# Rotary embedding on one core: whole-batch transfers, an earlier first load, and five tiles added or multiplied by other engines

## The chip, the cores and the metric

The kernel runs on one core of a Trainium2 chip. A core has five engines with queues of their own: PE (TensorE, matrix products into PSUM), DVE (VectorE), ACT (ScalarE), POOL (GpSimd) and SP (SyncE, used here only to issue transfers). Sixteen DMA engines move data between the main memory (HBM) and the on-chip memory (SBUF). PSUM is a second, smaller on-chip memory that PE writes and that DVE and ACT can read and write.

The metric is the device time of one execution in microseconds (us). Times are medians over several executions; what is profiled is one execution, whose span runs from its first to its last instruction.

## The reference

`x` has the shape (8, 2048, 8, 64), that is batch, position, head and feature, in float32: 33.5 MB. `cos` and `sin` are (2048, 32). For every position the two halves of a head's 64 features are rotated:

```python
x1 = x[..., : x.shape[-1] // 2]
x2 = x[..., x.shape[-1] // 2 :]
cos = cos[None, :, None, :]
sin = sin[None, :, None, :]
out1 = x1 * cos - x2 * sin
out2 = x1 * sin + x2 * cos
return np.concatenate([out1, out2], axis=-1)
```

The kernel must read 33.5 MB and write 33.5 MB, and do four multiplications and two additions for each pair.

## The kernel before

Each of the 128 partitions holds 16 consecutive positions of a batch. A position is `HD` = 512 floats (8 heads of 64), so a partition's row of one batch is 8192 floats (32 KB) that lie together in memory. A *slab* is half of such a row, 4096 floats or 16 KB in each of 128 partitions: 2 MB. There are 16 slabs, first the left halves of all eight batches, then the right halves. Ten slab buffers (`NBUF`) lie in SBUF. A slab is worked on in *units* of 2048 floats per partition (`UNIT`); the first slab in four smaller and larger pieces, and the last one too.

For each piece, `rotate` (line 97) issues four operations:

- POOL multiplies the second half of every head by sin and writes it where the first half's result goes, with the sign in the table (`nsin` is minus sin, line 91), and the first half by sin likewise: two multiplications of half the piece, line 107, into `t2` (SBUF, three buffers).
- DVE multiplies the whole piece by cos into `t1` (PSUM, one buffer), line 112. Its table `cos_ps` lies in PSUM, line 92.
- DVE adds `t1` and `t2` and writes the sum over the piece of `x`, line 117.

So the slab buffer becomes the output buffer. ACT issues the store of a slab once it is finished (line 127; the last slab is stored in four pieces), and SP issues the load of the slab ten places on, when the buffer's store has landed (lines 80 and 132). The tables are loaded first, sin on SP's queue (line 86) and cos on ACT's (line 87), then the first ten slabs on SP's queue. The semaphores are put in by the framework from the order in which tiles are written and read. A tile of a pool with `bufs` buffers takes the place of the tile `bufs` places before it, and waits until everything that reads that one has ended.[...]

Of the kernel before, what the change touches and what calls it, by code (L numbers as in the profile page):

```python
# [2 lines left out]

# [4 lines left out]


@with_exitstack  # L10
def kernel(
    ctx: ExitStack,
    tc: tile.TileContext,
    x: bass.AP,
    cos: bass.AP,
    sin: bass.AP,
    out: bass.AP,
):
    nc = tc.nc
    f32 = mybir.dt.float32  # L20
    PSUM = bass.MemoryType.PSUM

    B, S, H, D = x.shape
    Dh = D // 2
    P = 128
    HD = H * D
    R = S // P

    SL = 8
    n_half = R // SL  # L30
    SLAB = SL * HD
    UNIT = 4 * HD
    NBUF = 10

    xv = x.rearrange("b (q r) h d -> b q (r h d)", q=P)
    ov = out.rearrange("b (q r) h d -> b q (r h d)", q=P)
    cos_src = cos.rearrange("(q r) d -> q r d", q=P)
    sin_src = sin.rearrange("(q r) d -> q r d", q=P)

    const_pool = ctx.enter_context(tc.tile_pool(name="const", bufs=1))  # L40
    tab_pool = ctx.enter_context(tc.tile_pool(name="tab", bufs=1, space=PSUM))
    t1_pool = ctx.enter_context(tc.tile_pool(name="t1p", bufs=1, space=PSUM))
    xpool = ctx.enter_context(tc.tile_pool(name="xpool", bufs=NBUF))
    t2_pool = ctx.enter_context(tc.tile_pool(name="t2p", bufs=3))

    cos_sb = const_pool.tile([P, R, Dh], f32, tag="cb")
    sin_sb = const_pool.tile([P, R, Dh], f32, tag="sb")
    nsin = const_pool.tile([P, R, Dh], f32, tag="ns")
    cos_ps = tab_pool.tile([P, R, Dh], f32, tag="cp")

    slabs = [(b, l) for l in range(n_half) for b in range(B)]
    last = len(slabs) - 1
    xts = {}

    def cuts(i):
        if i == 0:
            return [HD, HD, 2 * HD, UNIT]
        return [SLAB]

    def pieces(i):  # L60
        if i == 0:
            return [HD, HD, 2 * HD, UNIT]
        if i == last:
            return [UNIT, 2 * HD, HD, HD]
        return [UNIT, UNIT]

    def stores(i):
        return pieces(i) if i == last else [SLAB]

    def spans(sizes):  # L70
        lo = 0
        for n in sizes:
            yield lo, n
            lo += n

    def load(i):
        b, l = slabs[i]
        xt = xpool.tile([P, SLAB], f32, tag="xt", name=f"xt{i}")
        for lo, n in spans(cuts(i)):
            nc.sync.dma_start(  # L80
                out=xt[:, lo : lo + n],
                in_=xv[b, :, l * SLAB + lo : l * SLAB + lo + n],
            )
        xts[i] = xt

    nc.sync.dma_start(out=sin_sb, in_=sin_src)  # L86
    nc.scalar.dma_start(out=cos_sb, in_=cos_src)
    for i in range(NBUF):
        load(i)

    nc.scalar.mul(nsin, sin_sb, -1.0)  # L91
    nc.vector.tensor_copy(cos_ps, cos_sb)  # L92

    def rep(a, n):
        return dataclasses.replace(a, ap=[a.ap[0][:], a.ap[1][:], [0, n], a.ap[-1][:]])

    def rotate(i, lo, n):
        b, l = slabs[i]
        xt = xts[i][:, lo : lo + n]
        r0 = l * SL + lo // HD  # L100
        nr = n // HD
        t1 = t1_pool.tile([P, n], f32, tag="t1")
        t2 = t2_pool.tile([P, n], f32, tag="t2")
        xu = xt.rearrange("p (g u d) -> p g u d", u=2, d=Dh)
        t2u = t2.rearrange("p (g u d) -> p g u d", u=2, d=Dh)
        for u, tab in ((1, sin_sb), (0, nsin)):
            nc.gpsimd.tensor_mul(  # L107
                out=t2u[:, :, u, :].rearrange("p (r h) d -> p r h d", h=H),
                in0=xu[:, :, 1 - u, :].rearrange("p (r h) d -> p r h d", h=H),
                in1=rep(tab[:, r0 : r0 + nr, :], H),  # L110
            )
        nc.vector.tensor_mul(  # L112
            out=t1.rearrange("p (r k d) -> p r k d", r=nr, d=Dh),
            in0=xt.rearrange("p (r k d) -> p r k d", r=nr, d=Dh),
            in1=rep(cos_ps[:, r0 : r0 + nr, :], 2 * H),
        )
        nc.vector.tensor_add(out=xt, in0=t1, in1=t2)  # L117

    for i, (b, l) in enumerate(slabs):
        done = 0  # L120
        st = list(spans(stores(i)))
        for lo, n in spans(pieces(i)):
            rotate(i, lo, n)
            done = lo + n
            while st and st[0][0] + st[0][1] <= done:
                slo, sn = st.pop(0)
                nc.scalar.dma_start(
                    out=ov[b, :, l * SLAB + slo : l * SLAB + slo + sn],
                    in_=xts[i][:, slo : slo + sn],
                )  # L130
        if i >= 1 and i - 1 + NBUF <= last:
            load(i - 1 + NBUF)


# [1 line left out]
_INS = ['x', 'cos', 'sin']  # L136
_OUTS = [((8, 2048, 8, 64), 'float32')]


# [23 lines left out]
```

## Time and profile before

| what | us |
|---|---|
| median of 9 runs (lowest, highest) | 164.95 (164.57, 165.22) |
| the profiled execution, device time | 164.97 |
| its span, first to last instruction | 163.2 |
| DVE busy in it | 148.8 |
| POOL busy in it | 147.7 |
| ACT busy in it | 1.9 |
| one DVE operation on 128x2048 (L112, L117) | 2.295, 2.292 |
| one POOL operation on 128x1024 (L107) | 2.33 |
| ACT, 128x512 (L91) | 0.63 |
| a 256 KB store at the end, issue to landing | 2.6 |

The profile's page gives the busy time of each engine, then the span in 40 slices of 4.08 us each (the busy share in tenths of every engine, and what the DMA engines moved), then a chain of waits: from the last instruction back to what released it, again and again, so that the shares say which engine held up the end. After that come groups of like instructions, by line: the engine, the operation, the tile written and the tile read, the number, the busy time in all, the mean duration of one in ns, and the engine's idle time just before them with what ended it. The timeline lists instructions in order of start: start, duration, engine, line.

The transfers moved 67.65 MB, 415 GB/s over the span.

### The profile page before, as it was taken

The page shows a single profiled execution, that of the slowest core. Times are in us where ns is not written, and L with a number is a line of the kernel's source. Part 1 is how long each engine was busy: PE and PEld are TensorE (multiplying, and loading weights), DVE is VectorE, ACT ScalarE, POOL GpSimd, SP SyncE. Part 2 cuts the span into 40 slices and gives each one's busy share as a digit, 9 for nine tenths or more (in the row PEclk, how much of TensorE's full clock was granted, in tenths as well). Part 3 has the DMA queues.
Part 4 walks back from the last instruction along what each step waited for, and adds up shares of the span by engine and source line. Part 5 has one row for each costly group of instructions (what it writes and reads, how often), then busy time and mean ns, then how long its engine had stood idle before and what let it go on. Part 6 is the DMA issues. An engine that isn't in the chain of part 4 may idle for free.

```text
span 163.2 us, 331 instructions
## 1 busy us (share of the span) xinstructions
DVE 148.8 (91%) x73; ACT 1.9 (1%) x2; POOL 147.7 (91%) x76
## 2 busy tenths in 40 slices
DVE  0687999999999999999999999999999999999992
ACT  3100000000000000000000000000000000000000
POOL 0799999999999999999999989999998998989720
DMA  5999999999999999999999999999999999999994
GB/s 157 359 444 434 402 394 434 434 434 426 434 434 418 442 434 430 430 434 428 418 442 438 426 426 442 428 418 442 442 418 426 446 426 422 442 430 430 426 410 193
DMA packets 5763, 67.65 MB, mean 415 GB/s; under 512 B 641, under 2 KB 641, under 8 KB 1665
## 3 DMA queue, kind: packets, MB, share of 16 engines
q1 hardware_dynamic: 2880, 33.82, 49.7%
q10 hardware_dynamic: 2880, 33.82, 48.6%
q14 instruction: 3, 0.02, 0.0%
HBM read 34.08 MB, written 33.55 MB: 414 GB/s over the span
## 4 chain that ended last, share of the span: by engine, by line
DVE 84%; DMA 7%; POOL 3%; issue 2%; SPq 1%; DVEq 0%; POOLq 0%
DVE xt L117 43%; DVE t L112 41%; DMA xt<-in_x_dram 7%; POOL t L107 3%; SPq L80 1%; DVEq L117 0%; SPq L86 0%; POOLq L107 0%
## 5 line engine op out<-in xcount | busy, mean ns | idle before, releaser
L107 POOL TENSOR_TENSOR t<-xt,sin_sb 128x1024 f32<-128x1024 f32 (+2 forms) x36 | 75.2, 2088 | 8.0 <-DMA xt<-in_x_dram 6.7
L117 DVE TENSOR_TENSOR xt<-t,t 128x2048 f32<-128x2048 f32 (+2 forms) x36 | 74.0, 2055 | 5.6 <-POOL t L107 2.4
L107 POOL TENSOR_TENSOR t<-xt,nsin 128x1024 f32<-128x1024 f32 (+2 forms) x36 | 75.3, 2090 | 0.0
L112 DVE TENSOR_TENSOR t<-xt,cos_ps 128x2048 f32<-128x2048 f32 (+2 forms) x36 | 74.1, 2058 | 1.2
L92 DVE COPY cos_ps<-cos_sb 128x512 f32<-128x512 f32 x1 | 0.7, 696 | 4.5 <-DMA cos_sb<-in_cos_dram 4.5
L91 ACT ACT_TABLE_LOAD x1 | 1.3, 1283 | 1.2 <-PEq L147 1.2
L91 ACT ACTIVATE nsin<-sin_sb 128x512 f32<-128x512 f32 x1 | 0.6, 629 | 1.8 <-DMA sin_sb<-in_sin_dram 1.8
L147 POOL MEMSET const-float32-0.0<- 128x1 f32 x1 | 0.1, 99 | 0.2 <-issue 0.2
L147 POOL MEMSET const-bfloat16-1.0<- 128x1 bf16 x1 | 0.1, 102 | 0.0
L147 POOL MEMSET const-uint8-127<- 128x1 uint8 x1 | 0.1, 102 | 0.0
L147 POOL MEMSET const-float32-1.0<- 128x1 f32 x1 | 0.1, 99 | 0.0
## 6 DMA issues: line engine op xcount, KB each, us to landing
xt<-in_x_dram SPq DMA_DIRECT2D x15, 2048.0 KB, 47.3
out_dram<-xt ACTq DMA_DIRECT2D x15, 2048.0 KB, 15.0
xt<-in_x_dram SPq DMA_DIRECT2D x1, 1024.0 KB, 7.7
out_dram<-xt ACTq DMA_DIRECT2D x1, 1024.0 KB, 5.3
xt<-in_x_dram SPq DMA_DIRECT2D x2, 256.0 KB, 4.2
xt<-in_x_dram SPq DMA_DIRECT2D x1, 512.0 KB, 5.6
out_dram<-xt ACTq DMA_DIRECT2D x1, 512.0 KB, 3.9
out_dram<-xt ACTq DMA_DIRECT2D x2, 256.0 KB, 2.6
```

Source lines behind the costliest of these rows:

```text
L80: nc.sync.dma_start(out=xt[:, lo : lo + n], in_=xv[b, :, l * SLAB + lo : l * SLAB + lo + n],)
L91: nc.scalar.mul(nsin, sin_sb, -1.0)
L92: nc.vector.tensor_copy(cos_ps, cos_sb)
L107: nc.gpsimd.tensor_mul(out=t2u[:, :, u, :].rearrange("p (r h) d -> p r h d", h=H), in0=xu[:, :, 1 - u, :].rearrange("p (r h) d -> p r h d" ...
L112: nc.vector.tensor_mul(out=t1.rearrange("p (r k d) -> p r k d", r=nr, d=Dh), in0=xt.rearrange("p (r k d) -> p r k d", r=nr, d=Dh), in1=rep ...
L117: nc.vector.tensor_add(out=xt, in0=t1, in1=t2)
L147: nc = _bacc.Bacc("TRN2", target_bir_lowering=False, num_devices=1)
```

## The change

The slabs of 2 MB become whole batches of 4 MB (32 KB a row) in five buffers, the same amount of SBUF. Batch 0 is loaded in pieces of 1, 1 and 2 MB, and worked on in two half units and three units; batch 7 is worked on in three units and two half units and stored in pieces of 2, 1 and 1 MB. All others are loaded and stored by one transfer each. The first 1 MB of `x` leads SP's queue, then cos and sin, both on SP's queue, then the rest. `keep` holds the operations of an engine in the written order.

Most units ("A") are computed as before. Five are not:

- "C", the first unit of batches 1 and 3: POOL does nothing. DVE multiplies the unit by cos (`t1`) and by sin (`t2`), both into the pool `t1s` in SBUF, which has two buffers. PE adds the right halves: a matmul of an identity matrix with a piece of `t1`, and one of the identity or its negative with a piece of `t2`, accumulated in PSUM (`o`, 128x512, two buffers). ACT copies each sum to `x`.
- "B", the second unit of batches 1 and 3 and the first of batch 5: POOL and DVE multiply as before, DVE into `t1s`; PE adds `t1` and `t2` through the identity, and ACT copies the sum to `x`.

The core of the diff:

```diff
-    NBUF = 10
+    NBUF = 5
+    C = 512
+    last = B - 1
...
+    o_pool = ctx.enter_context(tc.tile_pool(name="op", bufs=2, space=PSUM))
+    t1s_pool = ctx.enter_context(tc.tile_pool(name="t1s", bufs=2))
...
+    def load(b):
+        xt = xpool.tile([P, ROW], f32, tag="xt", name=f"xt{b}")
+        for lo, n in spans([UNIT, UNIT, 2 * UNIT] if b == 0 else [ROW]):
+            keep(nc.sync.dma_start(out=xt[:, lo : lo + n], in_=xv[b, :, lo : lo + n]))
+            if b == 0 and lo == 0:
+                keep(nc.sync.dma_start(out=cos_sb, in_=cos_src))
+                keep(nc.sync.dma_start(out=sin_sb, in_=sin_src))
+        xts[b] = xt
+
+    def store(b, lo, n):
+        keep(nc.scalar.dma_start(out=ov[b, :, lo : lo + n], in_=xts[b][:, lo : lo + n]))
...
+    keep(nc.scalar.mul(nsin, sin_sb, -1.0))
+    keep(nc.scalar.copy(sin_ps, sin_sb))
+    keep(nc.scalar.mul(neye, eye, -1.0))
+    keep(nc.vector.tensor_copy(cos_ps, cos_sb))
...
+    kinds = {}
+    for b in (1, 3):
+        kinds |= {(b, 0): "C", (b, UNIT): "B"}
+    kinds[(5, 0)] = "B"
+
+    def rotate(b, lo, n):
+        kind = kinds.get((b, lo), "A")
...
+        if kind == "A":
+            t1 = t1_pool.tile([P, n], f32, tag="t1")
+        else:
+            t1 = t1s_pool.tile([P, n], f32, tag="t1s")
+        if kind == "C":
+            t2 = t1s_pool.tile([P, n], f32, tag="t1s")
+        else:
+            t2 = t2_pool.tile([P, n], f32, tag="t2")
...
+        if kind != "C":
+            for u, tab in ((1, sin_sb), (0, nsin)):
+                keep(
+                    nc.gpsimd.tensor_mul(
...
+        if kind == "A":
+            keep(nc.vector.tensor_add(out=xt, in0=t1, in1=t2))
+        elif kind == "B":
+            for j in range(n // C):
+                o = o_pool.tile([P, C], f32, tag="o")
+                cs = slice(j * C, (j + 1) * C)
+                nc.tensor.matmul(o, eye, t1[:, cs], start=True, stop=False)
+                nc.tensor.matmul(o, eye, t2[:, cs], start=False, stop=True)
+                keep(nc.scalar.copy(xt[:, cs], o))
+        else:
+            keep(
+                nc.vector.tensor_mul(
+                    out=t2.rearrange("p (r k d) -> p r k d", r=nr, d=Dh),
+                    in0=xk,
+                    in1=rep(sin_ps[:, r0 : r0 + nr, :], 2 * H),
+                )
+            )
+            G = C // Dh
+            for u in range(2):
+                for j in range(n // 2 // C):
+                    o = o_pool.tile([P, C], f32, tag="o")
+                    gs = slice(j * G, (j + 1) * G)
+                    nc.tensor.matmul(o, eye, t1u[:, gs, u, :], start=True, stop=False)
+                    nc.tensor.matmul(
+                        o, eye if u else neye, t2u[:, gs, 1 - u, :], start=False, stop=True
+                    )
+                    keep(
+                        nc.scalar.copy(
+                            xu[:, gs, u, :], o.rearrange("p (g d) -> p g d", d=Dh)
+                        )
+                    )
+
+    def pieces(b):
+        if b == 0:
+            return [2 * HD, 2 * HD, UNIT, UNIT, UNIT]
+        if b == last:
+            return [UNIT, UNIT, UNIT, 2 * HD, 2 * HD]
+        return [UNIT] * 4
+
+    for b in range(B):
         done = 0
+        outs = list(spans([2 * UNIT, UNIT, UNIT] if b == last else [ROW]))
+        for lo, n in spans(pieces(b)):
+            rotate(b, lo, n)
             done = lo + n
+            while outs and sum(outs[0]) <= done:
+                store(b, *outs.pop(0))
+        if b + NBUF <= last:
+            load(b + NBUF)
```

## The prediction

> **What bounds the kernel now.** I read the page's first two parts, then its chain, then groups with shapes kept apart, then the ends of the timeline. Busy time first, with the slices:
>
> ```profile
> span 163.2 us, 331 instructions
> DVE 148.8 (91%) x73; ACT 1.9 (1%) x2; POOL 147.7 (91%) x76
> DMA  5999999999999999999999999999999999999994
> GB/s 157 359 444 434 402 394 434 434 434 426 434 434 418 442 434 430 430 434 428 418 442 438 426 426 442 428 418 442 442 418 426 446 426 422 442 430 430 426 410 193
> ```
>
> Three resources are full together: DVE and POOL at 91%, and the DMA engines, which move about 430 GB/s from the third slice to the last but one. ScalarE does nothing after the start, TensorE nothing at all. Which of the three ends last is in the chain of waits:
>
> ```profile
> DVE 84%; DMA 7%; POOL 3%; issue 2%; SPq 1%; DVEq 0%; POOLq 0%
> DVE xt L117 43%; DVE t L112 41%; DMA xt<-in_x_dram 7%; POOL t L107 3%; SPq L80 1%; DVEq L117 0%; SPq L86 0%; POOLq L107 0%
> ```
>
> DVE, two operations in turn. In time order, from the timeline:
>
> ```profile
> 4.23 0.63 ACT L91 ACTIVATE nsin<-sin_sb 128x512 f32<-128x512 f32 x1 [1.78 <-DMA sin_sb<-in_sin_dram]
> 5.28 0.72 POOL L107 TENSOR_TENSOR t<-xt,sin_sb 128x256 f32<-128x256 f32 x1 [4.84 <-DMA xt<-in_x_dram]
> ...
> 22.27 2.29 DVE L112 TENSOR_TENSOR t<-xt,cos_ps 128x2048 f32<-128x2048 f32 x1
> ...
> 24.67 2.29 DVE L117 TENSOR_TENSOR xt<-t,t 128x2048 f32<-128x2048 f32 x1
> ...
> 27.00 2.29 DVE L112 TENSOR_TENSOR t<-xt,cos_ps 128x2048 f32<-128x2048 f32 x1
> ...
> 154.54 1.23 DVE L112 TENSOR_TENSOR t<-xt,cos_ps 128x1024 f32<-128x1024 f32 x1
> ...
> 157.13 0.69 DVE L112 TENSOR_TENSOR t<-xt,cos_ps 128x512 f32<-128x512 f32 x1
> ...
> 159.45 0.69 DVE L117 TENSOR_TENSOR xt<-t,t 128x512 f32<-128x512 f32 x1
> ```
>
> From 27.00 minus 4.73 = 22.27 one reads the pitch: 4.73 us for a 128x2048 unit, 2.36 for each DVE operation with its gap. The first four units (8192 elements of a row) end at 26.96; DVE ends at 160.14, so 28 units take 133.2 us without a hole. The last store follows it by 3.06 us (163.2). POOL's pitch is smaller, 4.56 for two operations (its rows in the groups):
>
> ```profile
> L107 POOL TENSOR_TENSOR t<-xt,nsin 128x1024 f32<-128x1024 f32 x30 | 69.9, 2328 | 0.0
> L117 DVE TENSOR_TENSOR xt<-t,t 128x2048 f32<-128x2048 f32 x30 | 68.8, 2292 | 4.1 <-POOL t L107 1.3
> ```
>
> Outside the span lie 164.97 - 163.2 = 1.8 us in the profiled execution, whose 164.97 is also within 0.02 of the median of 9 runs.
>
> [...] the new multiplications have the same operands (x in SBUF, table in PSUM), so I price them at 2.36 with the gap.
>
> **Part by part.**
>
> *Start.* The first 1 MB of x now goes ahead of cos and sin on one queue. Before, sin landed at 4.23. Queried in short slices, the trace shows data flowing from 1.5 us, 0.2 MB by 3.0, then about 410 GB/s. So x's 1 MB is through at 3.0 + 0.85/0.41 = 5.1, cos and sin (0.26 MB each) at 6.35[...]. POOL, which started at 5.28, starts at 6.9: two half units of 2 x 1.24, then three units of 4.56, to 25.5. DVE's last addition of batch 0 then ends at 27.9, 0.95 later than 26.96. Building the identity, the negated identity and the second PSUM table lies beside the wait for data (ACT is idle, POOL was idle 4.84): nothing. The cos issue moves from ACT's queue to SP's, so two issues of 0.4 us now stand ahead of x's second piece: hidden, as x's first 2.4 us of data are under way.
>
> *DVE work removed.* The three B tiles lose their addition: 3 x 2.36 = 7.1 us. The C tiles lose none (two multiplications in place of one and an addition) but free POOL of two tiles, 9.1 us. The last batch ends in two half units, not one half and two quarters: two times (157.13 - 154.54) = 5.2 for 5.6, so 0.4 less. Without new waits DVE would end at 27.9 + 133.2 - 7.1 - 0.4 = 153.6.
>
> *The new wait.* C takes both t1s buffers; B, next in DVE's written order, needs the first. It is C's t1, read by the first, third, fifth and seventh of C's eight matmuls. So B's multiplication waits from C's second multiplication until the seventh matmul ends: the first can run early, six remain (second to seventh). Everything on DVE is queued behind it: the batch's two A tiles, and so the store. [...] S = 5.1 + 2.6 = 7.7 us. Bounds: six warm 5.2, six cold 10.3[...]. ScalarE's evacuation of 512 elements (0.63 by the nsin row) keeps up with two matmuls each and hides. Its copies stand on ACT behind the store of the batch before, which waits for DVE's last addition there; C's multiplications come after that addition too, so the order costs only the issue, 0.34 us, beside a matmul. There are two such places, batch 1 and batch 3: 2 x 7.7 = 15.4.
>
> *POOL behind TensorE.* t2 has three buffers, so the fourth POOL tile from a B needs that B's t2, which TensorE holds until its eighth matmul. In batches 1 and 3 TensorE comes warm from C: 2.4 + 8 x 0.86 + 4.6 of POOL = 13.9 us after B begins, and DVE wants it at 2.36 + 2 x 4.73 + 2.36 = 14.2: covered, by 0.3. All cold it would be 2.4 + 13.7 + 4.6 = 20.7, a stall of 6.5. In batch 5, B comes alone, TensorE cold: three cold and five warm, 9.4: 2.4 + 9.4 + 4.6 = 16.4 against 14.2, a stall of 2.2. It eats B's saving there.
>
> *Transfers.* A load or store of 4 MB in place of two of 2 MB moves the same bytes. At equal sharing (217 GB/s each way) store 0 runs from 27.9 to 47, load 5 follows it in the queue; batches 1 to 4 land before DVE reaches them (batch 2 by about 37, needed by POOL at 39), and later ones gain as DVE falls behind. So loads cost nothing here. What shows is the end: the last store is 1 MB, not 256 KB: 0.79 MB / 0.43 = 1.8 more, 4.9 us after DVE.
>
> *Sum.* 153.6 + 15.4 + 2.2 = 171.2, plus 4.9 = 176.1 span, plus 1.8 = 178.
>
> **Rivals.**
> - TensorE warm throughout[...]: S = 5.2, no stall in batch 5: 153.6 + 10.4 + 4.9 + 1.8 = 171. For it: the page's clock column reads 1.00 everywhere. Against: an unused engine shows nothing there.
> - Cold throughout[...]: 20.6 + 3 x 6.5: 153.6 + 40.1 + 6.7 = 200.[...]
> - The other side: one pass per matmul.[...] Then DVE ends at 156.2, and the span is 161.1, time 163. DMA allows about that: 67.65 MB / 0.434 = 155.9 plus 1.5 before the first byte and about 2 behind the last. It decides below S = (163.2 - 158.5)/2 = 2.35, that is 0.39 us a matmul. For it: no trace here shows the price.[...]
> - Transfers as the bound: if mixed 32 KB rows only reach the 398 GB/s of the fifth and sixth slices, 67.65 / 0.398 = 170, with 1.5 and 2 a span of 173.5, time 175. Against: later mixed slices reach 430.
>
> **How the numbers follow.** Forecast 0.54, warm 0.18, cold 0.12, one pass 0.10, transfers 0.06. Predicted 178; its own range 172 to 186. The range of 8 in 10, 168 to 190, leaves out one pass and most of the cold case. No change means within 0.2%, about what this kernel's measurement can tell; it has 0.02, out of the one-pass case, faster 0.08, slower 0.90.
>
> **What would show it.** In the changed profile: sin landing near 6.9 and the first store near 28; DVE idle about 7.7 us, released by PE, ahead of the first unit multiplication after each C in batches 1 and 3, nothing of it on loads; matmuls of 0.86 to 1.71 us; POOL idle on PE behind B, longest in batch 5; DMA slices with holes late; 4.9 us after DVE's end. I am wrong if matmuls take under 0.4 us, if DVE's idle time there names a load, or if transfers stay full to the end.

## The result, and the profile after

The changed kernel takes 172.58 us (median of 10 runs, 172.14 to 174.26), against 164.86 before (32 runs): a ratio of 1.048, 95% interval 1.046 to 1.050. 178 was predicted, from 168 to 190. The profiled execution took 173.84 us with a span of 171.8; it is one of the longer ones, so its sums are made against its own span.

From the page of the changed kernel, first busy times, then five of the rows by slices (4.3 us each):

```profile
span 171.8 us, 462 instructions
PE 43.1 (25%) x80; PEld 17.1 (10%) x80; DVE 140.5 (82%) x66; ACT 14.4 (8%) x24; POOL 138.6 (81%) x70
...
PE   0000000896950000099692000029800000000000
...
DVE  0477999606999999940999999999999999999980
...
PEclk9999999999997555559999555556995555555555
DMA  5999999999999999999999999999999970599955
GB/s 198 423 443 462 427 458 397 359 420 442 427 427 435 420 465 389 481 381 442 450 412 450 404 404 437 435 427 435 437 427 427 435 320 0 244 404 416 412 233 244
```

DVE and POOL each have 8 to 9 us less to do than before, and the time is longer all the same. DVE's row has two holes, a 0 in the ninth slice and one in the nineteenth, and each hole stands over a block of PE. The DMA row, full before to the last slice, now falls to nothing late (slice 34: 0 GB/s), though both kernels move the same 67.65 MB: transfers are no longer the bound. The view of waits (engine, line, what released it: us in all, times, longest) names the hole:

```profile
POOL t L122 <- DVE xt L136: 17.4, 2, 9.6
DVE t L129 <- PE o L157: 14.3, 2, 7.5
...
DVE xt L136 <- POOL t L122: 2.3, 2, 1.5
```

Line 129 is the multiplication by cos, line 157 the matmul on C's `t1`. It waits twice and for nothing else after the start. In batch 1 DVE starts nothing in these 7.51 us, although POOL is at work on the unit behind B from 34.73 on: its operations run in the written order here. POOL's 17.4 us follow from the same holes: it can go on only when an addition on DVE has read one of its buffers (2.7 us are left in a run below that has no such holes). In the timeline of batch 1 (start, duration; a row with x2 holds the two records that each fp32 matmul leaves here, 80 for 40 matmuls):

```profile
28.21 2.27 DVE L129 TENSOR_TENSOR t<-xt,cos_ps 128x2048 f32<-128x2048 f32 x1
...
30.41 2.28 DVE L146 TENSOR_TENSOR t<-xt,sin_ps 128x2048 f32<-128x2048 f32 x1
...
30.64 2.04 PE L157 MATMUL o<-t,eye 128*128 128x512 f32 x2 [30.64 <-DVE t L129]
...
32.84 2.05 PE L158 MATMUL o<-t,neye 128*128 128x512 f32 x2 [0.15 <-DVE t L146]
...
34.67 1.91 PE L157 MATMUL o<-t,eye 128*128 128x512 f32 x2
...
36.38 1.21 PE L158 MATMUL o<-t,neye 128*128 128x512 f32 x2
...
37.43 1.02 PE L157 MATMUL o<-t,eye 128*128 128x512 f32 x2
...
38.28 1.02 PE L158 MATMUL o<-t,eye 128*128 128x512 f32 x2
...
39.14 1.02 PE L157 MATMUL o<-t,eye 128*128 128x512 f32 x2
...
40.20 4.49 DVE L129 TENSOR_TENSOR t<-xt,cos_ps 128x2048 f32<-128x2048 f32 x2 [7.51 <-PE o L157]
```

The reader sees the six matmuls between the end of C's second multiplication (32.69) and the release: from start to start 1.83, 1.71, 1.05 us, then 0.86 a piece. The fourth on `t1` ends at 40.16, and B's multiplication starts at 40.20. In batch 3 the same wait is 6.76 us, and the first steps from start to start (75.17, 77.03, 78.23) are 1.86 and 1.20 us before they come down to 0.86. The PEclk row goes from half to full there, between slices 18 and 19. In what follows "cold" stands for a matmul at half clock (1.71 us from start to start) and "warm" for one at full clock (0.86). The row says nothing before its first step: it reads full in slice 8, where a matmul took 1.83 us, and the kernel before, which uses no TensorE, is given a mean clock of 1.00 too.

The end is as long as was worked out: DVE ends at 165.74 + 1.23 = 166.97, and the last 1 MB is stored 4.83 us later.

```profile
165.74 1.23 DVE L136 TENSOR_TENSOR xt<-t,t 128x1024 f32<-128x1024 f32 x1
```

One trap is in the chain of waits:

```profile
DVE 63%; DMA 17%; PE 8%; POOL 6%; issue 3%; SPq 0%; DVEq 0%; ACTq 0%; POOLq 0%
DVE t L129 32%; DVE xt L136 28%; DMA out_dram<-xt 14%; POOL t L122 6%; PE o L158 4%; PE o L157 4%; DMA sin_sb<-in_sin_dram 3%; DVE t L146 3%; DVEq L136 0%; SPq L69 0%; SPq L67 0%; ACTq L74 0%; POOLq L122 0%
```

14% go to a store, 23.2 us from 93.56, because batch 3's store lands at 116.79, just before an addition starts on DVE. The timeline shows that DVE worked through all of that stretch:

```profile
112.31 4.48 DVE L129 TENSOR_TENSOR t<-xt,cos_ps 128x2048 f32<-128x2048 f32 x2
...
116.25 2.34 POOL L122 TENSOR_TENSOR t<-xt,sin_sb 128x1024 f32<-128x1024 f32 x1
...
116.88 2.29 DVE L136 TENSOR_TENSOR xt<-t,t 128x2048 f32<-128x2048 f32 x1
```

The multiplications end at 116.79 and the addition starts at 116.88. The chain has taken one of two events of the same moment. No later load needs the buffer of batch 3, so its store held nobody up.

### The profile page after: what moved, and what is told of

Same layout as the page of the kernel before. It is cut to its first block, busy times and chain, and to the rows that moved or that the text cites. A ratio compares the mean times of both kernels' runs of the same rounds, so it can differ in the third digit from the quotient of the medians.

```text
span 171.8 us, 462 instructions
## 1 busy us (share of the span) xinstructions
PE 43.1 (25%) x80; PEld 17.1 (10%) x80; DVE 140.5 (82%) x66; ACT 14.4 (8%) x24; POOL 138.6 (81%) x70
## 2 busy tenths in 40 slices
DMA packets 3170, 67.65 MB, mean 394 GB/s; under 512 B 352, under 2 KB 352, under 8 KB 608
## 4 chain that ended last, share of the span: by engine, by line
DVE 63%; DMA 17%; PE 8%; POOL 6%; issue 3%; SPq 0%; DVEq 0%; ACTq 0%; POOLq 0%
DVE t L129 32%; DVE xt L136 28%; DMA out_dram<-xt 14%; POOL t L122 6%; PE o L158 4%; PE o L157 4%; DMA sin_sb<-in_sin_dram 3%; DVE t L146 3%; DVEq L136 0%; SPq L69 0%; SPq L67 0%; ACTq L74 0%; POOLq L122 0%
## 5 line engine op out<-in xcount | busy, mean ns | idle before, releaser
L122 POOL TENSOR_TENSOR t<-xt,sin_sb 128x1024 f32<-128x1024 f32 (+1 forms) x32 | 70.2, 2193 | 23.2 <-DVE xt L136 17.4
L129 DVE TENSOR_TENSOR t<-xt,cos_ps 128x2048 f32<-128x2048 f32 (+1 forms) x34 | 73.4, 2167 | 15.2 <-PE o L157 14.3
L122 POOL TENSOR_TENSOR t<-xt,nsin 128x1024 f32<-128x1024 f32 (+1 forms) x32 | 70.3, 2196 | 0.0
L136 DVE TENSOR_TENSOR xt<-t,t 128x2048 f32<-128x2048 f32 (+1 forms) x29 | 62.2, 2145 | 5.2 <-POOL t L122 2.3
L157 PE MATMUL o<-t,eye 128*128 128x512 f32 x16 | 11.5, 806 | 54.0 <-DVE t L129 54.0
L141 PE MATMUL o<-t,eye 128*128 128x512 f32 x24 | 13.6, 651 | 26.5 <-DVE t L129 26.5
L142 PE MATMUL o<-t,eye 128*128 128x512 f32 x24 | 13.1, 631 | 0.0
L143 ACT COPY xt<-o 128x512 f32<-128x512 f32 x12 | 7.0, 587 | 42.8 <-PE o L142 42.8
L162 ACT COPY xt<-o 128x512 f32<-128x512 f32 x8 | 4.7, 586 | 61.6 <-PE o L158 61.6
L157 PEld LDWEIGHTS o<-t,eye 128*128 128x128 f32 x16 | 3.9, 257 | 58.7 <-POOL t L122 30.6
L141 PEld LDWEIGHTS o<-t,eye 128*128 128x128 f32 x24 | 4.8, 212 | 33.8 <-issue 29.0
L158 PE MATMUL o<-t,neye 128*128 128x512 f32 x8 | 6.4, 887 | 0.2 <-DVE t L146 0.2
L142 PEld LDWEIGHTS o<-t,eye 128*128 128x128 f32 x24 | 4.9, 202 | 6.3 <-issue 6.3
L146 DVE TENSOR_TENSOR t<-xt,sin_ps 128x2048 f32<-128x2048 f32 x2 | 4.6, 2280 | 0.0
L158 PE MATMUL o<-t,eye 128*128 128x512 f32 x8 | 4.1, 592 | 0.0
L158 PEld LDWEIGHTS o<-t,neye 128*128 128x128 f32 x8 | 2.1, 287 | 5.0 <-issue 3.4
L158 PEld LDWEIGHTS o<-t,eye 128*128 128x128 f32 x8 | 1.5, 190 | 1.9 <-issue 1.9
```

The costliest lines, as they stand in the source:

```text
L122: nc.gpsimd.tensor_mul(out=t2u[:, :, u, :].rearrange("p (r h) d -> p r h d", h=H), in0=xu[:, :, 1 - u, :].rearrange("p (r h) d -> p r h d" ...
L129: nc.vector.tensor_mul(out=t1.rearrange("p (r k d) -> p r k d", r=nr, d=Dh), in0=xk, in1=rep(cos_ps[:, r0 : r0 + nr, :], 2 * H),)
L136: keep(nc.vector.tensor_add(out=xt, in0=t1, in1=t2))
L141: nc.tensor.matmul(o, eye, t1[:, cs], start=True, stop=False)
L142: nc.tensor.matmul(o, eye, t2[:, cs], start=False, stop=True)
L143: keep(nc.scalar.copy(xt[:, cs], o))
```

## The experiments

The theory is the prediction's: the time is lost where DVE waits for TensorE to let go of C's first buffer, and what the tiles save on DVE is smaller. Against it stand the coarse transfers, the half clock, and TensorE's work as such.

**All units "A".** The transfers, the start and the end of the changed kernel alone.

```diff
-    kinds = {}
-    for b in (1, 3):
-        kinds |= {(b, 0): "C", (b, UNIT): "B"}
-    kinds[(5, 0)] = "B"
+    kinds = {}
```

> All units are A; the rest is the changed kernel (4 MB transfers, its start and its end). Theory (the five tiles put in a wait of DVE on TensorE, 14.3 us, and save 8.3 us of DVE): DVE runs without a hole from batch 0's end at 28.3, 133.2 - 0.4 us more to 161.1, plus 4.8 of last store: span 165.9, time 167.7; no DVE idle above 1 us after 20 us. Rival (the whole-batch transfers cost the time, the five tiles gain): time 173 or more, DVE idle on loads or store landings.

168.04 us, ratio 1.019 (1.017 to 1.021); DVE ends at 161.57 in a span of 166.4. So the five tiles cost 4.5 us of the change's 7.7, and the rest of the change costs 3.2.

**The same with the start and the end of the kernel before**, so that the size of the transfers, and with it the order of the half batches, is the main difference that is left. Batch 0's pieces also become those of the kernel before.

```diff
-            return [UNIT, UNIT, UNIT, 2 * HD, 2 * HD]
+            return [UNIT, UNIT, UNIT, 2 * HD, HD, HD]
...
-        outs = list(spans([2 * UNIT, UNIT, UNIT] if b == last else [ROW]))
+        outs = list(spans([UNIT, UNIT, UNIT, 2 * HD, HD, HD] if b == last else [ROW]))
...
+    keep(nc.sync.dma_start(out=sin_sb, in_=sin_src))
+    keep(nc.scalar.dma_start(out=cos_sb, in_=cos_src))
     for b in range(NBUF):
         load(b)
```

> All units A as in e1_all_a, with the start and the end of the kernel before (tables first on two queues, x in 256 KB pieces, last stores of 512, 256 and 256 KB), so that only the 4 MB transfers differ from the kernel before. Theory: 4 MB transfers cost nothing while DVE sets the end: 164.6 to 165.2, against 168.04 with the changed start and end. Rival (coarse transfers cost by themselves): 166 or more.

164.95 us, ratio 1.002 (1.001 to 1.003). All but about 0.3 us of the 3.2 (0.2 to 0.5 by the interval) are thus the start and the end, and 4 MB transfers cost no more than that rest while DVE sets the end.

**C without B, and the three B without C.**

```diff
+    kinds = {(1, 0): "C", (3, 0): "C"}
```

> Only the C units of batches 1 and 3, no B: the same matmuls on C's products, but nobody needs their buffer soon. Theory (the loss is B's wait, not C): no DVE wait on PE, DVE as in the kernel with all units A less 2 x 0.2, time 167.3 to 168.0. Rival (C itself costs): 173 or more.

167.41 us, ratio 1.018 (1.014 to 1.021), 0.6 us less than with all units A: no loss from C. In its profiled execution (168.90 us) TensorE went slower than anywhere else, 5.3 us a matmul from start to start:

```profile
37.27 5.63 PE L154 MATMUL o<-t,eye 128*128 128x512 f32 x2
42.56 5.63 PE L155 MATMUL o<-t,neye 128*128 128x512 f32 x2
47.85 5.63 PE L154 MATMUL o<-t,eye 128*128 128x512 f32 x2
```

C's eight matmuls then lasted from 30.68 to about 69, and DVE, with no B behind, waited for TensorE 1.5 us in all (for the buffers of the second C). A slow TensorE alone doesn't make this loss; a wait on it does: 5.3 us a matmul cost DVE 1.5 us here, and 0.86 to 1.86 us a matmul cost it 14.3 in the changed kernel.

```diff
+    kinds = {(1, UNIT): "B", (3, UNIT): "B", (5, 0): "B"}
```

> The two C units become A, the three B stay: B's buffers are free when it comes. Theory: no wait of DVE on TensorE; DVE ends at 161.1 - 3 x 2.36 - 3 x 0.15 = 153.6, span 158.5 by DVE, but DMA needs 67.65/0.43 = 157.3 and 3.5 around it, so 160.5 to 161; time 162.5, faster than before by 1.4%. Rival (an addition on TensorE costs by itself, by half clock or by holding POOL's buffer): time stays near 170, with POOL idle on TensorE behind each B.

164.73 us, ratio 0.9995 (0.998 to 1.001). The wait on TensorE is gone and the time comes down by 3.3 us against all-A, but 162.5 was missed. From the page's chain, and the view of waits:

```profile
POOL 57%; DVE 30%; issue 6%; DMA 3%; SPq 0%; DVEq 0%; POOLq 0%
```

```profile
DVE xt L133 <- POOL t L119: 7.4, 5, 2.0
```

B takes an addition from DVE and nothing from POOL. POOL has all its 32 units to do, at 4.56 us each, and holds most of the chain; DVE gives more than half of its 7.1 us back in waits on it (7.4 us, where the run with all units A has 2.5). C is what relieves POOL, and the two belong together.

**C and B in the same batch, but apart.** The same operations, B two units later.

```diff
-        kinds |= {(b, 0): "C", (b, UNIT): "B"}
+        kinds |= {(b, 0): "C", (b, 3 * UNIT): "B"}
```

> Batches 1 and 3 run C, A, A, B in place of C, B, A, A; same operations. Theory: two A units (9.4 us of DVE) lie over the 7.5 us in which TensorE reads C's first buffer, so the wait goes: DVE ends near 152.7, span again set by DMA at 160.5 to 161, time 162.5. Rival (what costs is TensorE's time or clock wherever it stands, the wait moves to ScalarE and the store): time 168 or more, store 1 later than 52.

163.89 us, ratio 0.994 (0.992 to 0.996): 8.7 us faster than the changed kernel, and 0.9 us faster than the kernel before, a small difference but clear of the noise. Its view of waits has no entry of DVE on PE. DVE ends at 153.0, as expected, and the span is 162.1, because the DMA engines are now full to the end. From its page and the end of DVE's timeline:

```profile
span 162.1 us, 459 instructions
...
DMA  5999999999899999999999998998999999999994
GB/s 186 410 439 501 404 404 493 340 396 437 388 477 429 396 477 420 396 493 404 420 485 388 429 471 388 437 469 388 439 469 396 453 445 404 453 437 400 420 414 196
```

```profile
151.78 1.22 DVE L136 TENSOR_TENSOR xt<-t,t 128x1024 f32<-128x1024 f32 x1
```

Nine microseconds lie between DVE's last operation and the end. 162.5 was expected. The middle runs at the 430 GB/s that was assumed (from 8.1 to 154 us); the first and the last slice, at 186 and 196 GB/s, lose 4.5 us between them where 3.5 were assumed, and that is most of the difference.

**Apart, with finer last stores.**

```diff
-            return [UNIT, UNIT, UNIT, 2 * HD, 2 * HD]
+            return [UNIT, UNIT, UNIT, 2 * HD, HD, HD]
...
-        outs = list(spans([2 * UNIT, UNIT, UNIT] if b == last else [ROW]))
+        outs = list(spans([UNIT, UNIT, UNIT, 2 * HD, HD, HD] if b == last else [ROW]))
```

> C, A, A, B as in e3_apart, with the last batch's work and stores cut as in the kernel before (last store 256 KB). Theory: DMA sets the end there, its queue is full when DVE ends at 153, so finer last stores gain nothing: 163.9 within 0.3. Rival (the tail after DVE is still the bound): 162.1.

163.98 us, ratio 0.996 (0.995 to 0.997): no gain. The same 1 MB store that costs 1.8 us behind a DVE-bound end (4.83 us from DVE's end to the end of the span in the changed kernel, 3.06 in the kernel before) costs nothing behind a full queue.

**A third buffer, order unchanged.** The room for it came from `t2`.

```diff
-    t1s_pool = ctx.enter_context(tc.tile_pool(name="t1s", bufs=2))
+    t1s_pool = ctx.enter_context(tc.tile_pool(name="t1s", bufs=3))
...
-    t2_pool = ctx.enter_context(tc.tile_pool(name="t2p", bufs=3))
+    t2_pool = ctx.enter_context(tc.tile_pool(name="t2p", bufs=2))
```

> Order C, B, A, A unchanged, but a third buffer in the pool of C's and B's products, paid with one of GpSimd's three t2 buffers[...]. Theory: B no longer waits for C's matmuls, DVE idles less than 2 us on PE in all, DVE ends near 154, DMA sets the end: time 163.5 to 165. Rival (the wait isn't for that buffer but for TensorE's sums or the bank of its output): both waits of 7 us stay and the time is 172 or more.

186.47 us, ratio 1.132 (1.130 to 1.135): far from what was expected. The wait did go: B's multiplication now starts at 32.74, right behind C's, and DVE waits nowhere on PE. But the waits on its view are others:

```profile
POOL t L122 <- DVE xt L136: 31.9, 12, 4.8
DVE xt L136 <- POOL t L122: 31.0, 14, 2.4
```

In its timeline after B, one multiplication and one addition at a time:

```profile
46.75 2.33 POOL L122 TENSOR_TENSOR t<-xt,sin_sb 128x1024 f32<-128x1024 f32 x1 [2.40 <-DVE xt L136]
...
51.39 2.29 DVE L136 TENSOR_TENSOR xt<-t,t 128x2048 f32<-128x2048 f32 x1 [2.39 <-POOL t L122]
53.72 2.29 DVE L129 TENSOR_TENSOR t<-xt,cos_ps 128x2048 f32<-128x2048 f32 x1
53.76 2.32 POOL L122 TENSOR_TENSOR t<-xt,sin_sb 128x1024 f32<-128x1024 f32 x1 [2.40 <-DVE xt L136]
```

POOL starts each of these units only when DVE's addition has read the unit just before it, and DVE waits for that unit in turn: 53.76 - 46.75 = 7.0 us a unit in place of 4.7. The two engines behave as if only one of the two `t2` buffers were in use. TensorE reads B's until 47.9, but the unit that starts at 53.76 still waited; why it didn't take the buffer that TensorE had left isn't shown. The run settles that the wait was for the buffer, since B ran ahead of the six matmuls; its time tells nothing on the change, because the two `t2` buffers were a second edit with a price of its own.

**More TensorE work in C, and a warmer TensorE.**

```diff
+                    nc.tensor.matmul(o, eye, t1u[:, gs, u, :], start=True, stop=True)
                     nc.tensor.matmul(o, eye, t1u[:, gs, u, :], start=True, stop=False)
```

> In C each matmul on t1 is issued twice (the second overwrites the first), so three more matmuls stand between C's second multiplication and the release of its first buffer, at 0.86 us warm. Theory: each wait of DVE grows from 7.1 to 9.7 us, the time by 5.2 us to 177.8. Rival (TensorE's work is beside the path): within 0.5 us of the changed kernel's 172.6.

179.65 us, ratio 1.088 (1.083 to 1.094); 7.1 us above the changed kernel, 5.9 between the two spans (the changed kernel's profiled execution is 1.3 above its median). 5.2 were expected. In the profiled execution the waits grew from 14.3 to 20.2, that is by the same 5.9:

```profile
DVE t L129 <- PE o L158: 20.2, 2, 10.3
```

```diff
+            pre = xts[b - 1][:, 2 * UNIT : 2 * UNIT + C]
+            for _ in range(6):
+                o = o_pool.tile([P, C], f32, tag="o")
+                nc.tensor.matmul(o, eye, pre, start=True, stop=True)
             G = C // Dh
```

> Six more matmuls, whose sums nobody reads, run on TensorE from about 4.7 us before each C, so that its clock is up when C's matmuls come. Theory (the wait is six matmuls, some at half clock): each wait shrinks to 6 x 0.86 = 5.2 us, time 172.6 - 2 x 1.9 = 168.8. Rival (the clock is not what prices the wait, or TensorE's queue is): 172 to 174.

169.83 us, ratio 1.032 (1.029 to 1.036); its waits:

```profile
DVE t L129 <- PE o L161: 9.9, 2, 5.1
```

168.8 was expected. The matmuls of C are warm from the first on (two in 1.88 us, where the first alone took 2.04 in the changed kernel). But their order has changed too, since TensorE's are not held in the written order (a row with x4 holds two matmuls):

```profile
30.89 1.88 PE L161 MATMUL o<-t,eye 128*128 128x512 f32 x4
...
32.88 1.95 PE L162 MATMUL o<-t,neye 128*128 128x512 f32 x4
...
34.67 1.11 PE L161 MATMUL o<-t,eye 128*128 128x512 f32 x2
...
36.47 1.02 PE L161 MATMUL o<-t,eye 128*128 128x512 f32 x2
```

Two matmuls on `t1` (L161) now run before the first on `t2` (L162), so five matmuls stand in the wait of batch 1, not six. The edit thus does two things. In the changed kernel's trace the six matmuls last 7.3 and 6.7 us, and at 0.86 from start to start they would last 5.3: the low clock is 3.3 of the 14.3 us. The other 1.1 us by which the waits fell to 9.9 are the order. About 11 of the 14.3 us stay with a warm TensorE.

**Batch 5 without its B.**

```diff
-    kinds[(5, 0)] = "B"
```

> The changed kernel with batch 5's first unit as A in place of B. If that B saved its DVE addition in full (no wait of GpSimd behind it, as the trace of the changed kernel reads): 172.6 + 2.5 = 175.1. If, as the prediction had it, 2.2 us of it went to a stall of GpSimd behind TensorE: 172.8.

175.41 us, ratio 1.066 (1.062 to 1.069), 2.8 above the changed kernel: this B saved its addition in full.

**The same placement in the kernel before.** 2 MB slabs, C in the first unit of slabs 2 and 6, B in the second unit of slabs 3 and 7 and the first of slab 10.

```diff
+    kinds = {(2, 0): "C", (3, UNIT): "B", (6, 0): "C", (7, UNIT): "B", (10, 0): "B"}
```

> The kernel before (2 MB slabs, its start and end) with five tiles placed so that no wait arises: C in the first unit of slabs 2 and 6, B in the second unit of slabs 3 and 7 and the first of slab 10. Theory: DVE would end near 152.5, DMA sets the end as in e3_apart: 163.5 to 164.2. If 4 MB transfers gave the gain of e3_apart: 164.7 as before.

164.81 us, ratio 1.000 (0.998 to 1.002), although DVE ends at 154.1. That is not the 163.5 to 164.2 of the theory: the placement alone gives nothing with 2 MB slabs. The last run gave it the changed kernel's start:

```diff
-            return [HD, HD, 2 * HD, UNIT]
+            return [UNIT, UNIT]
...
-            return [HD, HD, 2 * HD, UNIT]
+            return [2 * HD, 2 * HD, UNIT]
...
+            if i == 0 and lo == 0:
+                keep(nc.sync.dma_start(out=cos_sb, in_=cos_src))
+                keep(nc.sync.dma_start(out=sin_sb, in_=sin_src))
```

> e11_slabs (2 MB slabs, no wait on TensorE, last stores small) with the changed kernel's start: x's first 1 MB ahead of both tables on one queue. If the start gives e3_apart its 0.9 us (its rows of 8 KB moved 295 GB/s in the first 8 us against 258 with rows of 2 KB, about 0.3 MB or 0.7 us, and 0.2 MB more in the next 8 us): 163.6 to 164.1. If the rows of 32 KB give it: 164.8 as e11_slabs.

164.74 us, ratio 0.999 (0.998 to 1.000). The start is not it, and the size of the last stores was not it either, so the 0.9 us come with the whole-batch transfers. The page's queue rows (packets, MB, share of 16 engines' span), first with 2 MB slabs, then with whole batches in the kernel with C and B apart:

```profile
q1 hardware_dynamic: 2736, 34.08, 50.0%
q10 hardware_dynamic: 2736, 33.56, 48.2%
```

```profile
q1 hardware_dynamic: 1728, 34.08, 49.9%
q10 hardware_dynamic: 1440, 33.56, 48.0%
```

98.2% of 163.0 is 160.1 us, 97.9% of 162.1 is 158.7: the same bytes in 2304 packets fewer keep the 16 engines busy for 1.4 us less. Whether that is a price for each packet, or the later and longer overlap of loads and stores, these runs don't tell.

## Why the prediction was right, point by point

The direction and the main mechanism were right: a wait took more than the removed additions gave. The sum came out 5.4 us high, nearly all of its errors to one side.

- **Start.** Sin was to land at 6.9, 6.35 for its data and the rest the author's estimate; POOL's first multiplication started at 7.07. Batch 0's last addition was to end at 27.9; it ended at 28.29.
- **The new wait.** 15.4 us were forecast in two places; 14.3 came, in those two places, released by the matmul named. The 7.7 us a wait, 5.1 for three cold matmuls and 2.6 for three warm, were the author's estimate, since the kernel before has no matmul. This trace shows the two prices that they imply, 1.71 cold and 0.86 warm. Both lie above the 0.39 us a matmul below which the one-pass rival would have decided. What was off is the number of cold ones. Batch 1 shows two cold, one between and three warm, batch 3 one cold, one between and four warm. The forecast let its 5.1 us at half clock run from C's second multiplication, but the slow matmuls run from the first one, which starts 2.2 us earlier (30.64 against 32.84). TensorE reached its full clock about 6 us after the first matmul in batch 1, by the steps of its matmuls, and 4.7 and 3.9 in batches 3 and 5, by the granted clock (0.50 to 1.00 at 77.7 and 118.7), so the 5.1 itself lay near their mean of 4.9. The warm rival's 171 is nearer to 172.58 than 178 is, but not for its reason: TensorE wasn't warm throughout. It had right that no stall would come in batch 5.
- **DVE work removed.** 7.1 + 0.4 us were counted. From 28.29, 133.2 us less 0.4 plus the 14.27 of waits make 175.36, and DVE ended at 166.97, so 8.4 us went in place of 7.1. Where an operation on DVE doesn't depend on the one before it, as at C and B, the two start 2.20 us apart (28.21 and 30.41), not the 2.36 counted. There are eight such places: a multiplication behind a multiplication five times, and behind an addition three times (26.00 and 28.21). Together they are about 1.25 of the 1.3 us.
- **POOL behind TensorE: the step that failed.** A stall of 2.2 us in batch 5 was forecast, because the third POOL unit behind B was held to take B's own `t2` buffer, which TensorE reads until its last matmul. Its 9.4 us for the eight matmuls, three cold and five warm, were an estimate too; they took 9.1 (114.73 to 123.79). No stall came:

```profile
120.87 2.35 POOL L122 TENSOR_TENSOR t<-xt,sin_sb 128x1024 f32<-128x1024 f32 x1
...
122.77 1.02 PE L142 MATMUL o<-t,eye 128*128 128x512 f32 x2
```

That unit started at 120.87, while TensorE was still at work on B, until 123.79. It had got an A unit's buffer, which the addition that started at 116.88 had read by 119.17. The buffers of a pool are thus not taken strictly in turn, and the description of the kernel before, by which a tile takes the place of the one `bufs` places back, is wrong in this. POOL ran without a gap from 88.84 on, and where it waited, in batches 1 and 3, DVE's addition of an A unit released it (17.4 us), never TensorE. The run without this B shows the saving whole, 2.8 us. A stall of this kind can come all the same: with C and B apart, POOL waited for TensorE once, 0.9 us.
- **Transfers and end.** Loads cost nothing, as said, and the DMA engines had holes late. The tail was 4.83 for 4.9.

With the waits gone the forecast had 163 in its one-pass rival, and 163.89 was measured, but that is in part luck: DVE was to set the end there, at 161.1, and the transfers were to allow 159.4 (155.9 + 1.5 + 2, the 2 behind the last byte an estimate). It was the transfers that set it, at 162.1. The 32 KB rows gained little: the better version's whole gain over 2 MB slabs is 0.5%. Its slices between the first and the last show from 340 to 501 GB/s, so one slice is no measure of the rate; over 146 us both that version and the kernel before moved 430.

Summed, the predicted end of DVE, 171.2, less 2.2 (no stall), less 1.1 (shorter waits), less 1.3 (DVE work, the part left over), plus 0.4 (start), is 167.0, where the trace has 166.97. The median execution lies another 1.3 us below the profiled one; no trace shows where.

## What to carry to other kernels

Work moved to an idle engine wasn't free when something near behind needed its buffers (14.3 us of waits here): count what still reads a buffer when the next tile of the pool is due, and put enough other work between (two units of 4.7 us over a wait of 7.5 turned a loss of 4.8% into a gain of 0.6%). Moving work off one of two engines that are both nearly full gained less than half of it (3.3 of 7.1 us) before the other was relieved too. Then a third limit, here the DMA engines, took over: DVE ended 7 us earlier than in the kernel before, and the time came down by 0.9. The size of the last store had a price only under the bound that it stood behind: 1.8 us behind DVE, nothing behind a full queue.

## What the runs showed of the hardware

- An fp32 matmul of 128x512 shows as two records with a weight load each, 0.43 us apart warm and 0.86 cold. In the changed kernel TensorE reached its full clock about 4 to 6 us after the first matmul in batches 1, 3 and 5 and lost it again between the batches, in batch 1 some 4 us after the last matmul (49.7 to about 54, where the granted clock falls from 1.00 to 0.50).
- In the execution profiled with C alone TensorE took 5.3 us a matmul, three times the cold price of 1.71, for over 70 us, and the profile has no row of the granted clock there. Why is open.
- One buffer fewer in a pool between two engines of nearly equal pace cost more than all else tried, 186 us: for stretches the two engines took turns, 7.0 us a unit in place of 4.7.
- Two operations of 128x2048 on DVE that don't depend on each other start 2.20 us apart, a dependent multiplication and addition 2.40, though each takes about 2.29.
